# A two-layer trunk on one core: pair sums on POOL, a longer start on one half of the input, one attention pipeline, and tokens on partitions at the end

## The chip, the core and the metric

The kernel runs on one core of a Trainium2 chip. A core has a matrix engine (TensorE, PE in the profile; its weight loads are PEld), a vector engine (VectorE, DVE), a scalar engine (ScalarE, ACT), a general engine (GpSimd, POOL) and a synchronization engine (SyncE, SP) that here only issues DMA transfers. They run side by side, each in the order of its own queue, and wait for one another through semaphores. PE writes its results into eight banks of PSUM, each of 128 partitions by 512 fp32 numbers. The metric is the device time of one execution in microseconds.

## The reference

Input `x` is (1, 512, 1024) in fp32: 512 tokens, 1024 channels. There are two layers; all arithmetic is fp32.

```python
h = x
# layer 0
h = h + conformer_conv(rmsnorm(h, norm_mix[0]), ...)  # a = glu(x @ w_pw1 + b_pw1); y = causal depthwise
                                                      # conv of 31 taps; y = silu(layernorm(y)); y @ w_pw2 + b_pw2
h = h + swiglu_ffn(rmsnorm(h, norm_ffn[0]), w_up[0], w_down[0])   # (silu(x@gate) * (x@up)) @ down, 2816 hidden
k, v = split(rmsnorm(h, norm_kv) @ w_kv)              # 4 heads of 64, shared
# layer 1
q = rmsnorm(h, norm_mix[1]) @ w_q                     # 16 heads of 64
h = h + banded_sink_attention(q, k, v, sinks, rel_bias) @ w_o     # window of 128, blocks of 128 queries
h = h + swiglu_ffn(rmsnorm(h, norm_ffn[1]), w_up[1], w_down[1])
return rmsnorm(h, norm_final)
```

`rmsnorm(x, g)` is `x * rsqrt(mean(x * x) + 1e-6) * g` over the channels. In the attention every block of 128 queries sees its own and the previous block of keys; a learned sink takes part in the maximum and the sum of the softmax.

## The kernel before

**Layout.** `h` is held with channels on partitions: eight tiles of 128 channels by 512 tokens. A matmul takes a 128 x 128 piece of a weight as its stationary operand and a tile of activations, 256 or 512 tokens wide, as its moving one.

**Three matmuls for one product.** Weights come as 512 KB chunks, in the order of a list (`chunk_plan`). Six chunks ahead of use one is fetched by SP; three ahead ACT makes its high part (`whi`, L203) and DVE its low part (`wlo`, L204). Activations are split the same way (L382 and L383 with the norm's gain, L386 and L387 elsewhere). `mm3` then issues three matmuls, high by high (L262), high by low (L263), low by high (L264), in the format fp32r, a cheaper pass than plain fp32. Sums over channels are plain fp32 matmuls with a matrix of ones.

**Layer 0** goes by two halves of 256 tokens as far as its FFN's first part (channel pairs 0 to 4 of 11; the rest runs at 512 tokens). The convolution's 31 taps are shared: DVE does some into a PSUM bank (L611), for the others ACT multiplies (L603) and POOL adds (L604); POOL adds the two results (L615). Tiles go two at a time; such a pair also gets its squares (ACT) and its sums for the layer norm: four matmuls with `ones_m`, two of y and two of the squares (`sums`, L649). Half two's convolution is a generator (`background`) that is advanced by a few steps at each weight chunk while PE runs half one's `pw2` and FFN part; squares follow four steps, sums eight steps behind a pair's end. DVE also has the residual (L731), the eight L383 and the running sum of squares (L340) of half one's norm at that time.

**The norm** is not applied before the FFN. `Rms.step1` sums the squares over channels (L350), DVE adds the epsilon (L352), POOL takes the power of −1/2 (L354), ACT puts the result on a diagonal (L362), and `step2` spreads it to all partitions by a matmul (L375). The evacuation of a pair of FFN channels multiplies by it.

**FFN.** `ffn_up` takes a pair's gate and up products over eight input tiles, in two chunks each of four tiles (`half` 0: tiles 0 to 3, `half` 1: tiles 4 to 7). At 256 tokens the first pair waits for evacuation until the next pair's first half.

**Attention** has 16 units (two head groups x four blocks x two), each a chain of steps: scores on 64 rows (L928), bias and minimum on DVE (L931), exponentials on ACT (L938), division on POOL (L942), transposes by PE (L950) with a split on ACT and DVE, then the product with V. Two row groups of PE, rows 0 to 63 and 64 to 127, hold two heads each. A `pipeline` of eight units lets the steps of five units overlap; it has 12 steps. The first pipeline is advanced within the second half of the query projection (8 steps) and then finished with nothing between, the second one likewise within the output projection's first part.

**The end.** `Fin` finishes the last down projection (channel pairs 9 and 10) half by half of the tokens, with channels on partitions; squares, sums by `ones_c` matmuls, L1072 on POOL, a spread (L1084), and products on DVE and POOL into an output of shape (1024, 512), which the host transposes.

The order of each engine's queue is set by a scheduler that works from the order of the program and its own estimates, with `tc.issue_after` where the code asks for one thing behind another.

Of the kernel before, what the change touches and what calls it, by code (L numbers as in the profile page):

```python
# [10 lines left out]
F32 = mybir.dt.float32  # L11
# [38 lines left out]

def chunk_plan():
# [16 lines left out]
    for _ in range(2):  # L68
        pw2()
        ffn(0, *HALVES0[0])  # L70
# [17 lines left out]
    for hf in range(2):  # L88
        for kp in range(*LAST):
            for g in range(2):  # L90
                plan.append(("down", 1, kp, g))
# [58 lines left out]
def hybrid_trunk(ctx: ExitStack, tc: tile.TileContext, xT, W, prm_in, wdw_in, sinks, relb, onehot, outT):  # L150
# [115 lines left out]
    class Act:  # L266
# [5 lines left out]
        def __getitem__(self, i):  # L272
            a, b = self.q[i // self.per]
            return a[:, i % self.per, :], b[:, i % self.per, :]

# [129 lines left out]
    def down_group(keys, act_of, banks, on_step=None):  # L405
        nk = len(keys)
        w = banks[0].shape[-1]
        for ci, (key, kts) in enumerate(keys):
# [10 lines left out]
            if on_step is not None and ci == nk - 1:  # L419
                on_step()  # L420
                on_step()

    def ffn_part(layer, part, xg, tok, rms, on_h=None):
        lo, hi = (HALVES0, HALVES1)[layer][part]
        hid = ffn_up(layer, lo, hi, xg, tok, rms)
        w = tok.stop - tok.start
        for g in range(2):
            if w == 256:
# [22 lines left out]
    def ffn_up(layer, lo, hi, xg, tok, rms):  # L451
        w = tok.stop - tok.start
        hid = Act(2 * (hi - lo), w)

        def evac(pair, banks):
            rs_bc = rms.step2()
            if w == 256:
# [17 lines left out]
        pending = []  # L475
        for pair in range(lo, hi):
            if w == 256:
                full = [bank(), bank()]
                banks = [b[:, e * w:(e + 1) * w] for b in full for e in range(2)]
            else:  # L480
                full = banks = accs(w)
            for half in range(2):
                for which in range(2):
                    whi, wlo = get("up", layer, pair, half, which)
                    order = [(k, m) for k in range(4) for m in range(2)]
                    if half == 1:
                        order = [(k, m) for m in range(2) for k in range(4)]
                    for k, m in order:
                        sl = slice(m * P, (m + 1) * P)
                        mm3(banks[which * 2 + m], (whi[:, k, sl], wlo[:, k, sl]), cut(xg[half * 4 + k], tok),  # L490
                            half == 0 and k == 0 and opens(m, w), half == 1 and k == 3 and closes(m, w))
                    if half == 0 and which == 1:
                        if w == 512:
                            rms.step1()
                        for p in pending:
                            evac(*p)
                        pending = []
            if w == 256 and pair == lo:
                rms.step1()
                pending.append((pair, full))  # L500
            else:
                evac(pair, full)
# [45 lines left out]
    with tc.tile_pool(name="conv", bufs=2) as cv:  # L548
# [29 lines left out]
        class Half:  # L578
# [246 lines left out]
        x0 = {"ffn0": Act(KT)}  # L825
# [3 lines left out]
        ffn_part(0, 0, x0["ffn0"], HALF[0], n0.rms)  # L829
# [17 lines left out]
    ffn_part(0, 0, x0["ffn0"], HALF[1], n1.rms)  # L847
# [11 lines left out]
    if True:  # L859
# [45 lines left out]
        def q_evac(g, banks):  # L905
# [263 lines left out]
```

## Time and profile before

| | |
|---|---|
| three runs | 1115.78, 1115.91 (median), 1117.93 us |
| the profiled execution | 1115.77 us, of it 1114.0 us from the first to the last instruction (the span) |
| mean clock that TensorE was granted | 0.993 |
| busy share of the span: PE, PEld, DVE, ACT, POOL | 99%, 86%, 59%, 45%, 29% |
| chunks fetched / split | 202 / 194 |
| bytes moved by DMA | 125.00 MB, mean 112 GB/s |

A row of a timeline has its start in microseconds, its length, the engine, the line of the kernel, the operation, what it writes and reads, their form, and the number of instructions folded into the row; brackets at its end give the idle time just before it and what ended that. A row of a group has the count, then the busy time of all, the mean nanoseconds of one, then the idle time before them. A plain fp32 matmul leaves two records in the trace, a matmul in fp32r one. Records of matmuls overlap, so the pace is read from the starts. A slice of the span in the page's second part is 27.9 us.

### The profile page before, as it was taken

The numbers are of one execution on the slowest core, as the hardware profiler recorded it, in microseconds if no ns is written. First come the engines' busy times: TensorE is split into PE (matmuls) and PEld (weight loads), VectorE is DVE, ScalarE is ACT, GpSimd is POOL, SyncE is SP. The second block draws the span as 40 slices with busy tenths as digits, with TensorE's granted clock in tenths as the row PEclk, the third lists the DMA queues.
The fourth block names the chain that finished last, engine by engine and source line by source line (L and its number), as shares of the span: only waits on it lengthen the run. The fifth ranks groups of instructions, "written<-read, shape, count | busy, mean of one in ns | idle before, by whom it ended". The sixth has DMA issues, their size and how long they took to land.

```text
span 1114.0 us, 15803 instructions
## 1 busy us (share of the span) xinstructions
PE 1098.9 (99%) x5994; PEld 955.7 (86%) x5994; DVE 662.3 (59%) x1074; ACT 502.6 (45%) x891; POOL 322.1 (29%) x420
## 2 busy tenths in 40 slices
PE   9999998999999999999999999999999999999997
PEld 8888898999999888888888788888888888888886
DVE  4999999977665454443575686683444333444455
ACT  4786787765543232232343574553322211332233
POOL 4999699700100021110230332241111100110014
PEclk9999998999999999999999999999999999999998
DMA  9227044576655423332322201023233333323332
GB/s 362 100 31 84 25 168 136 183 247 190 189 174 184 135 95 101 105 97 95 95 95 87 75 29 48 30 95 95 95 95 95 97 102 103 96 95 95 95 95 77
DMA packets 40857, 125.00 MB, mean 112 GB/s; under 512 B 4395, under 2 KB 12748, under 8 KB 40780
## 3 DMA queue, kind: packets, MB, share of 16 engines
q1 hardware_dynamic: 40204, 123.55, 36.2%
q8 instruction: 47, 0.77, 0.3%
q10 hardware_dynamic: 576, 0.44, 0.1%
q14 instruction: 30, 0.25, 0.1%
HBM read 118.73 MB, written 5.24 MB: 111 GB/s over the span
## 4 chain that ended last, share of the span: by engine, by line
PE 90%; DVE 5%; ACT 2%; issue 1%; POOL 1%; DMA 0%; SPq 0%; POOLq 0%; DVEq 0%; ACTq 0%
PE bank L263 26%; PE bank L262 26%; PE bank L264 26%; PE bank L562 8%; PE bank L928 1%; DVE quad L383 1%; PE bank L649 1%; ACT pr L603 1%; DVE bank L611 1%; PE bank L950 1%; DVE wlo L204 1%; DMA h<-in_xT_dram 0%; DVE sc L931 0%; PE bank L375 0%; DVE ptl L954 0%
## 5 line engine op out<-in xcount | busy, mean ns | idle before, releaser
L263 PE MATMUL bank<-quad,whi 128*128 128x512 f32 (+1 forms) x1536 | 535.2, 349 | 3.8 <-DVE quad L383 3.7
L262 PE MATMUL bank<-quad,whi 128*128 128x512 f32 (+1 forms) x1536 | 534.8, 350 | 0.5 <-ACT quad L968 0.5
L264 PE MATMUL bank<-quad,wlo 128*128 128x512 f32 (+1 forms) x1536 | 535.1, 348 | 0.0
L204 DVE TENSOR_TENSOR wlo<-raw,whi 128x1024 fp32r<-128x1024 f32 x194 | 262.5, 1354 | 322.4 <-ACT whi L203 312.3
L203 ACT CAST whi<-raw 128x1024 fp32r<-128x1024 f32 x194 | 203.3, 1049 | 360.0 <-PE bank L263 319.3
L263 PEld LDWEIGHTS bank<-quad,whi 128*128 128x128 f32 x1536 | 292.0, 190 | 40.9 <-DVE quad L383 5.0
L262 PEld LDWEIGHTS bank<-quad,whi 128*128 128x128 f32 x1536 | 291.7, 190 | 38.5 <-ACT quad L968 0.9
L264 PEld LDWEIGHTS bank<-quad,wlo 128*128 128x128 f32 x1536 | 292.1, 190 | 36.8 <-issue 0.2
L472 POOL TENSOR_TENSOR tmp<-tmp,tmp 128x512 f32<-128x512 f32 x34 | 48.4, 1425 | 486.7 <-DVE tmp L471 473.1
L604 POOL TENSOR_TENSOR pr<-pr,pr 128x256 f32<-128x256 f32 x208 | 161.6, 825 | 11.0 <-ACT pr L603 11.0
L611 DVE SCALAR_TENSOR_TENSOR bank<-apad,wdw,bank 128x256 f32<-128x256 f32 x248 | 113.2, 485 | 3.6
L562 PE MATMUL bank<-quad,w 128*128 128x256 f32 x512 | 114.2, 382 | 0.6 <-DMA w<-in_W_dram 0.5
L562 PEld LDWEIGHTS bank<-quad,w 128*128 128x128 f32 x512 | 97.4, 191 | 15.4 <-DVE quad L537 1.7
L603 ACT ACTIVATE pr<-apad,wdw 128x256 f32<-128x256 f32 x208 | 99.0, 503 | 20.8 <-POOL pr L604 18.1
L340 POOL TENSOR_TENSOR tmp<-tmp,tmp 128x256 f32<-128x256 f32 (+1 forms) x35 | 38.8, 1109 | 138.6 <-ACT tmp L336 109.1
L470 ACT ACTIVATE tmp<-tmp 128x512 f32<-128x512 f32 x34 | 21.4, 632 | 92.9 <-DVE tmp L469 92.9
L942 POOL TENSOR_SCALAR sc<-sc,sm 128x256 f32<-128x256 f32 (+1 forms) x64 | 30.0, 489 | 79.4 <-DVE sm L940 79.4
L386 ACT CAST quad<-tmp 128x512 fp32r<-128x512 f32 (+1 forms) x50 | 29.1, 586 | 30.4 <-POOL tmp L472 26.6
L471 DVE TENSOR_TENSOR tmp<-bank,rsbc 128x512 f32<-128x512 f32 x34 | 23.5, 691 | 32.4 <-PE bank L264 32.4
L383 DVE SCALAR_TENSOR_TENSOR quad<-h,prm,quad 128x512 fp32r<-128x512 f32 (+1 forms) x40 | 39.5, 1020 | 0.5 <-ACT quad L382 0.4
L938 ACT ACTIVATE sc<-sc,m 128x257 f32<-128x257 f32 (+1 forms) x64 | 30.3, 476 | 15.4 <-DVE m L931 13.7
L387 DVE TENSOR_TENSOR quad<-tmp,quad 128x512 fp32r<-128x512 f32 (+1 forms) x50 | 32.8, 661 | 2.5 <-ACT quad L386 2.5
(140 smaller groups left out, 747.0 us busy)
## 6 DMA issues: line engine op xcount, KB each, us to landing
raw<-in_W_dram SPq DMA_DIRECT2D x202, 512.0 KB, 3.5
w<-in_W_dram SPq DMA_DIRECT2D x15, 512.0 KB, 9.7
fd<-fs SPq DMA_DIRECT2D x1, 3072.0 KB, 33.8
h<-in_xT_dram SPq DMA_DIRECT2D x8, 256.0 KB, 5.9
bias<-fd SPq DMA_DIRECT2D x8, 256.0 KB, 5.5
out_dram<-res SPq DMA_DIRECT2D x14, 128.0 KB, 1.8
w<-in_W_dram SPq DMA_DIRECT2D x2, 256.0 KB, 4.1
out_dram<-res ACTq DMA_DIRECT2D x2, 128.0 KB, 2.7
```

Source lines behind the costliest of these rows:

```text
L203: nc.scalar.copy(hi, r)
L204: lo_engine[0].tensor_sub(lo, r, f32(hi))
L262: nc.tensor.matmul(out, w[0], x[0], start=start, stop=False)
L263: nc.tensor.matmul(out, w[0], x[1], start=False, stop=False)
L264: nc.tensor.matmul(out, w[1], x[0], start=False, stop=stop)
L340: self.eng.tensor_add(sq, self.acc, sq)
L383: nc.vector.scalar_tensor_tensor(dst[1], src, g, f32(dst[0]), op0=ALU.mult, op1=ALU.subtract)
L472: nc.gpsimd.tensor_mul(t2, t1, t2)
L562: mm = nc.tensor.matmul(self.pb[:, w * W2:(w + 1) * W2], w1[ct][:, w, k, :], x[k] if x else xg[k][:, tok], start=k == 0, stop=k == KT - 1)
L603: on_act = nc.scalar.mul(pr, a[:, j:j + W2], tap(j))
L604: on_pool = nc.gpsimd.tensor_add(pr, acc, pr)
L611: on_dve = nc.vector.scalar_tensor_tensor(yt if i == nd - 1 else c, src, tap(i), c if i else self.shift, op0=ALU.mult, op1=ALU.add)
```

## The change

Five things are changed.

1. For half two of the convolution (`hf` is 1), `sums` has POOL add the two y tiles of a pair into a new tile `yy` (one buffer) and the two squares in place; one matmul with `ones_m` for each sum takes the place of two.
2. FFN part one of half two is made in a `twin` form: the high and low parts of an activation stand side by side (`Pairs`), so that the high weights multiply both in one 512-wide matmul, and the low weights the high part in one of 256 (`mm2`). The two column halves of a bank are added in the evacuation.
3. FFN part one of half one takes its chunks `ahead`: first tiles 0 to 3 of pairs 0 and 1, then tiles 4 to 7 of both. Pairs 0 and 1 are evacuated after the latter.
4. Attention is one pipeline of 16 units and 20 steps: 8 within the second half of the query projection, 4 with nothing between, 8 within the output projection's first part. The second half's queries are evacuated bank by bank. The twelve score matmuls of a unit are held in strict turn between the two row groups by `issue_after`, behind a tiny matmul (1 x 1) into one of their banks.
5. At the end the activations are the stationary operand and the weights the moving one, 512 wide, so that tokens lie on partitions: a `Block` of 128 tokens gets its part of `h` by eight transposes into PSUM, then the products on top. ACT squares with a running sum, POOL takes the power for 128 tokens at once, and ACT and DVE multiply by it. `norm_final` is fetched by SP as a broadcast of 512 KB. The last four chunks are fetched once, not twice (198 fetched and 190 split).

```diff
-    def ffn(layer, lo, hi):
-        for pair in range(lo, hi):
-            for half in range(2):
-                for which in range(2):
-                    plan.append(("up", layer, pair, half, which))
+    def ffn(layer, lo, hi, ahead=False):
+        for pair, half in up_order(lo, hi, ahead):     # ahead: o[1], o[2] = o[2], o[1]
+            for which in range(2):
+                plan.append(("up", layer, pair, half, which))
...
+    def mm2(out, w, x, start, stop):
+        first, second = (w[0], x, out), (w[1], x[:, 0, :], out[:, 0, :])
+        if stop:
+            first, second = second, first
+        nc.tensor.matmul(first[2], first[0], first[1], start=start, stop=False)
+        nc.tensor.matmul(second[2], second[0], second[1], start=False, stop=stop)
...
+                for which, t in enumerate((t1, t2)):
+                    for m in range(2):
+                        b = banks[which * 2 + m]
+                        tm = t[:, m * w:(m + 1) * w]
+                        nc.scalar.copy(tm, b[:, 1, :])
+                        nc.vector.tensor_add(tm, b[:, 0, :], tm)
...
+                if self.hf:
+                    for f, (t, u) in enumerate(((self.y[:, 2 * p, :], self.y[:, 2 * p + 1, :]), self.sq)):
+                        both = u
+                        if f == 0:
+                            both = cv.tile([P, W2], F32, tag="yy", name=uid("yy"), bufs=1)
+                        nc.gpsimd.tensor_add(both, t, u)
+                        mm = nc.tensor.matmul(self.st[:, f * W2:(f + 1) * W2], ones_m, both,
+                                              start=p == 0 and f == 0, stop=p == KT // 2 - 1 and f == 1)
+                    return mm.ins
...
-        ffn_part(0, 0, x0["ffn0"], HALF[0], n0.rms)
+        ffn_part(0, 0, x0["ffn0"], HALF[0], n0.rms, ahead=True)
...
-    ffn_part(0, 0, x0["ffn0"], HALF[1], n1.rms)
+    ffn_part(0, 0, x0["ffn0"], HALF[1], n1.rms, twin=True)
...
+            mm = nc.tensor.matmul(pbs[1][0:1, 0, 0:1], ones_c, ones_c, start=True, stop=True)
...
-                        nc.tensor.matmul(pbs[g][:, e, :], qs[gp][a][rows[g], j, qt],
-                                         kq[rows[g], b, gp, k0:k0 + BAND], start=a + b == 0, stop=a == 1)
+                        with tc.issue_after(mm.ins):
+                            mm = nc.tensor.matmul(pbs[g][:, e, :], qs[gp][a][rows[g], j, qt],
+                                                  kq[rows[g], b, gp, k0:k0 + BAND], start=a + b == 0, stop=a == 1)
...
-            units = [unit(gp, jp, n) for n in range(NBLK) for jp in range(2)]
+            units = [unit(gp, jp, n) for gp in range(2) for n in range(NBLK) for jp in range(2)]
...
+            for i in range(KT):
+                c = (i % 4) * P
+                nc.tensor.matmul(self.banks[i // 4][:, c:c + P], h[i][:, self.tok], ident, is_transpose=True,
+                                 start=i % 4 == 0, stop=False)
...
+                for n, (x, w) in enumerate(((a[0], whi), (a[0], wlo), (a[1], whi))):
+                    nc.tensor.matmul(self.banks[g], x, w[:, k, :], start=False, stop=kp == LAST[1] - 1 and k == 1 and n == 2)
...
+            nc.scalar.activation(sq, b, AF.Square, accum_out=ss[:, g:g + 1])
...
+                nc.gpsimd.tensor_tensor(rs, ss[:, 3:4], mhalf[:, 0:1], op=ALU.pow)
```

The scheduler moves more than these lines say. Line numbers of the changed kernel are higher: taps are L686 (DVE) and L679 (POOL), splits L209, L409 stands for L383 and L366 for L340, L267 to L269 for the three matmuls, L401 for the spread, L690 for the sum of both parts of y.

DVE where half one's norm input is made, before (`wlo_1732` is the low part of the fifth FFN chunk):

```order
L204 TENSOR_TENSOR wlo_1686<-raw_1529,whi_1685 128x1024
L383 SCALAR_TENSOR_TENSOR quad_1318<-h,prm,quad_1317 128x256
L340 TENSOR_TENSOR tmp_1606<-tmp_1477,tmp_1606 128x256
L383 SCALAR_TENSOR_TENSOR quad_1318<-h,prm,quad_1317 128x256 x2
L340 TENSOR_TENSOR tmp_1612<-tmp_1606,tmp_1612 128x256
L383 SCALAR_TENSOR_TENSOR quad_1318<-h,prm,quad_1317 128x256
L340 TENSOR_TENSOR tmp_1618<-tmp_1612,tmp_1618 128x256
L340 TENSOR_TENSOR tmp_1624<-tmp_1618,tmp_1624 128x256
L204 TENSOR_TENSOR wlo_1732<-raw_1573,whi_1731 128x1024
L204 TENSOR_TENSOR wlo_1770<-raw_1633,whi_1769 128x1024
```

And in the changed kernel (`wlo_1736` is the same place in the list of chunks):

```order
L209 TENSOR_TENSOR wlo_1688<-raw_1530,whi_1687 128x1024
L409 SCALAR_TENSOR_TENSOR quad_1317<-h,prm,quad_1317 128x256
L366 TENSOR_TENSOR tmp_1613<-tmp_1607,tmp_1613 128x256
L686 SCALAR_TENSOR_TENSOR bank_1489<-apad_158,wdw,bank_1489 128x256
L409 SCALAR_TENSOR_TENSOR quad_1318<-h,prm,quad_1318 128x256 x2
L366 TENSOR_TENSOR tmp_1619<-tmp_1613,tmp_1619 128x256
L686 SCALAR_TENSOR_TENSOR y_1020<-apad_157,wdw,bank_1489 128x256
L686 SCALAR_TENSOR_TENSOR y_1020<-apad_158,wdw,bank_1489 128x256
L686 SCALAR_TENSOR_TENSOR bank_1857<-apad_159,wdw,bank_1270 128x256
L366 TENSOR_TENSOR tmp_1625<-tmp_1619,tmp_1625 128x256
L209 TENSOR_TENSOR wlo_1736<-raw_1574,whi_1735 128x1024
L686 SCALAR_TENSOR_TENSOR bank_1857<-apad_160,wdw,bank_1270 128x256
```

Taps now stand between the norm's rows, the first tap of the next pair among them; the fifth chunk's low part still follows all of the norm's rows.

POOL behind pair 2's last tap (`y_1020` is half two's convolution result), before:

```order
L604 TENSOR_TENSOR pr_1785<-pr_1777,pr_1785 128x256
L615 TENSOR_TENSOR y_1020<-y_1020,pr_1781 128x256
L615 TENSOR_TENSOR y_1020<-y_1020,pr_1785 128x256
L354 TENSOR_TENSOR rs_1818<-ms_1816,mhalf 128x2
L604 TENSOR_TENSOR pr_1911<-pr_1866,pr_1911 128x256
```

and in the changed kernel, where L726 is the new pair of adds:

```order
L679 TENSOR_TENSOR pr_1789<-pr_1781,pr_1789 128x256
L690 TENSOR_TENSOR y_1020<-y_1020,pr_1785 128x256
L690 TENSOR_TENSOR y_1020<-y_1020,pr_1789 128x256
L679 TENSOR_TENSOR pr_1904<-pr_1858,pr_1904 128x256
L679 TENSOR_TENSOR pr_1908<-pr_1861,pr_1908 128x256
L726 TENSOR_TENSOR yy_2109<-y_1020 128x256
L679 TENSOR_TENSOR pr_1912<-pr_1904,pr_1912 128x256
L679 TENSOR_TENSOR pr_1916<-pr_1908,pr_1916 128x256
L380 TENSOR_TENSOR rs_1893<-ms_1891,mhalf 128x2
L679 TENSOR_TENSOR pr_1950<-pr_1912,pr_1950 128x256
L726 TENSOR_TENSOR sq_2015<-sq_2013,sq_2015 128x256
```

Taps of pair 3 and the norm's power now stand between pair 2's y and the two new adds.

PE at pair 2's sums, in the changed kernel:

```order
L267 MATMUL bank_1732<-quad_1318,whi_1853 128x256
L268 MATMUL bank_1732<-quad_1318,whi_1853 128x256
L269 MATMUL bank_1732<-quad_1318,wlo_1854 128x256
L727 MATMUL bank_1376<-yy_2109,ones_m 128x256
L727 MATMUL bank_1376<-sq_2015,ones_m 128x256
L401 MATMUL bank_1982<-tmp_1895,ones_m 128x256
L267 MATMUL bank_1997<-quad_1315,whi_1900 128x256
```

Before, the spread of the norm (L375) stood 77 rows of matmuls ahead of the pair's four sums; now the two sums stand directly ahead of it, in front of the third pair's first chunk.

More of the change, by code (lines that the diff above doesn't have):

```diff
@@ L48, with up_order @@
 NPARAM = _c
+def up_order(lo, hi, ahead):
+    o = [(pair, half) for pair in range(lo, hi) for half in range(2)]
+    if ahead:
+        o[1], o[2] = o[2], o[1]
+    return o
 def chunk_plan():
@@ L149, in hybrid_trunk @@
 @with_exitstack
[L150 removed]
+def hybrid_trunk(ctx: ExitStack, tc: tile.TileContext, xT, W, prm_in, wdw_in, sinks, relb, onehot, fin, out):
     nc = tc.nc
@@ L473, in evac @@
                 split(hid[2 * (pair - lo) + m], t2)
[L475 to L498, printed above, removed]
```

297 lines of the change are left out of this document (159 added, 138 removed).

## The prediction, made before the changed kernel ran

> **What bounds the kernel now.** I read the page's busy times first, then the chain of waits, then busy times by stretches, then the timelines of the stretches where TensorE (PE) is not full.
>
> ```profile
> PE 1098.9 (99%) x5994; PEld 955.7 (86%) x5994; DVE 662.3 (59%) x1074; ACT 502.6 (45%) x891; POOL 322.1 (29%) x420
> PEclk9999998999999999999999999999999999999998
> PE 90%; DVE 5%; ACT 2%; issue 1%; POOL 1%; DMA 0%; SPq 0%; POOLq 0%; DVEq 0%; ACTq 0%
> ```
>
> PE is busy for 99% of the span and carries 90% of the chain. So the time is PE's work, plus the few places where PE stands still or is clocked down, plus the end. Only slice 7 of the clock (167 to 195 us) and the last one fall short. By stretches (length, then busy time and count of PE, PEld, DVE, ACT, POOL, then granted clock, DMA share, GB/s):
>
> ```profile
> 160.00:180.00 20.00, 17.03 (x110) 16.18 (x109) 19.82 (x27) 17.16 (x36) 20.00 (x21) 0.83 0.50 171
> 180.00:220.00 40.00, 40.00 (x328) 39.74 (x328) 36.05 (x54) 30.95 (x54) 33.46 (x34) 1.00 0.54 170
> 270.00:290.00 20.00, 20.00 (x169) 20.00 (x168) 17.82 (x23) 12.69 (x23) 5.78 (x7) 1.00 0.58 182
> 640.00:660.00 20.00, 19.66 (x140) 17.18 (x139) 19.05 (x55) 16.40 (x49) 9.09 (x20) 1.00 0.14 49
> ```
>
> At 160 to 180 us PE is idle for 20.00 − 17.03 = 2.97 us and the clock costs 20 × 0.17 = 3.4 us: 6.4 us are lost, the largest prize in the program. DVE (19.82) and POOL (20.00) are both full there. At 180 to 220 us PE loses nothing, and POOL still has 6.5 us free.
>
> **The convolution sums and the new order of chunks, 150 to 230 us.** These belong together, because both decide what PE waits for in one stretch.
>
> ```profile
> 161.06 0.47 PE L262 MATMUL bank<-quad,whi 128*128 128x256 f32 x1
> 169.16 0.39 PE L263 MATMUL bank<-quad,whi 128*128 128x256 f32 x1 [1.88 <-DVE quad L383]
> 170.90 0.58 PE L263 MATMUL bank<-quad,whi 128*128 128x256 f32 x1 [0.99 <-DVE quad L383]
> 168.16 0.94 DVE L383 SCALAR_TENSOR_TENSOR quad<-h,prm,quad 128x256 fp32r<-128x256 f32 x1
> 175.13 3.42 DVE L204 TENSOR_TENSOR wlo<-raw,whi 128x1024 fp32r<-128x1024 f32 x2
> 197.54 1.73 PE bank L649 x8
> 225.18 1.73 PE bank L649 x8
> ```
>
> A plain fp32 matmul leaves two records, so the eight of a pair's sums are four matmuls: 1.73 / 4 = 0.43 us each. Half two loses eight of its sixteen: 8 × 0.43 = 3.45 us of PE work gone.
>
> The stall is PE at tiles 4 to 7 of the normalized input, which DVE (L383) finishes late. With the new order PE first does four chunks that need tiles 0 to 3 alone: 4 × 24 matmuls × 0.12 us (next part) = 11.5 us of work before it needs the rest; now the two chunks from 161.06 are all it has. But the fifth chunk also needs its own low part. In the changed order on DVE that split still stands behind every tile's L383 and L340 work, with one tap more ahead of it. Before, the two splits ran from 175.13, so the first was done near 176.8; one tap (36.05 / 54 bounds it by 0.67 us) makes that about 177.3. PE comes there at 161.06 − 0.86 (two sums of pair 1 saved) + 11.5 = 171.7 us. So the wait changes its name, from the tile to the low weights, and I do not book the 6.4 us.
>
> The second half is POOL's queue.
>
> ```profile
> 156.55 26.37 POOL L604 TENSOR_TENSOR pr<-pr,pr 128x256 f32<-128x256 f32 x26
> 182.88 2.41 POOL L615 TENSOR_TENSOR y<-y,pr 128x256 f32<-128x256 f32 x2
> 185.25 0.71 POOL L354 TENSOR_TENSOR rs<-ms,mhalf 128x2 f32<-128x2 f32 x1
> L604 POOL TENSOR_TENSOR pr<-pr,pr 128x256 f32<-128x256 f32 x208 | 161.6, 825 | 11.0 <-ACT pr L603 11.0
> 220.54 2.42 POOL L615 TENSOR_TENSOR y<-y,pr 128x256 f32<-128x256 f32 x2 [7.09 <-DVE y L611]
> ```
>
> A tap of POOL takes 26.37 / 26 = 1.01 us here, and I take 0.9 us for a 128x256 add of two tiles (the mean over all taps is 0.825). POOL was running without a gap from 156.55. In the changed order pair 2's squares come out of POOL at 156.55 + 26.37 (taps) + 1.8 (pair 1's two adds) + 2.41 (two y) + 2.0 (two taps) + 0.9 (yy) + 2.0 + 0.71 (pow) + 1.0 (tap) + 0.9 (squares) = 194.6 us. On PE, the last sum of pair 2 now stands 7.5 us of work nearer the start than the first one did: 1.7 us is the four matmuls saved at pairs 0 and 1, and 5.8 us its move ahead by some 50 rows. So PE gets there at 197.54 − 7.5 = 190.0 us if the old stall stays as it is, and at 183.6 if it goes: in both cases it waits for POOL until 194.6. Behind that sum on PE stand the spread of the norm (L401) and all further chunks, and ACT and DVE wait for their banks. From there to any later point PE has 7.5 us of moved or saved work to count, less the whole saving of 3.45: 194.6 + 7.5 − 3.45 − 197.54 = +1.1 us. I take **+1.0 us**. From below the bound is −3.45 − 6.4 = −9.9 (no stall left), from above two further stretches at half clock, +6.8, and a later POOL.
>
> The trace's half clock lasts one stretch worth 3.4 us, after PE had been idle 1.88 and 0.99 us within 2.7. The Trainium skill ("TensorE: Matmul & The Clock Gate", Part 1) says that the gate looks at free-running windows of about 3.4 us and halves the clock after an idle one; by that figure a cold window would cost an estimated 1.7 us, half of what this row shows, so the measurement decides and the row's 3.4 us is used.
>
> **The twin form, half two's first FFN part.** 240 triples (5 pairs × 4 chunks × 8, plus 10 chunks × 8) become a 512-wide and a 256-wide matmul each.
>
> ```profile
> 269.75 0.28 PE L264 MATMUL bank<-quad,wlo 128*128 128x256 f32 x1
> 289.91 0.28 PE L264 MATMUL bank<-quad,wlo 128*128 128x256 f32 x1
> 399.71 0.39 PE L262 MATMUL bank<-quad,whi 128*128 128x512 f32 x1
> 419.88 0.39 PE L264 MATMUL bank<-quad,wlo 128*128 128x512 f32 x1
> ```
>
> Starts give the pace: 20.16 us over 168 matmuls is 0.120 us at 256 wide, 20.17 over 89 is 0.2266 at 512. A triple goes from 0.360 to 0.3466, so 240 × 13.4 ns = 3.2 us go. The evacuation grows (four copies, four adds, two products on POOL); at 270 to 290 us DVE is busy 17.82 of 20, ACT 12.69 and POOL 5.78, so there is room beside PE, least of it on DVE, where two products with the norm go and four adds come. The norm is now asked for after half a pair, not a whole one, and its spread stands on PE only a few triples behind; a wait there is −0 to 1.5 us. I take **−2.4 us**, bounds −3.2 and 0.
>
> **Attention.** PE runs scores of 64 rows, two groups at once.
>
> ```profile
> 616.25 0.90 PE bank L928 x12
> 628.36 0.90 PE bank L928 x6
> 629.68 0.90 PE bank L928 x6
> 749.62 0.79 PE bank L350 x8
> 697.19 0.57 issue
> 699.68 0.88 ACT sc L938 x3
> 700.59 1.17 ACT sc L938 x5
> ```
>
> Twelve scores in turn between the two row groups take 0.90 us; six of one group by themselves take 0.90 too. Where the order separated the groups a unit costs 0.88 us more. About four and a half of sixteen units read like 628.36: strict turn saves 4.5 × 0.88 = 3.95 us. The tiny matmul ahead of each unit is plain fp32 of one column; four of them took 0.79 us (L350 with 8 records), so 16 × 0.2 = 3.2 us at most and about 1 us if only its issue shows; I take 2.4. One pipeline has one fill and one drain. The chain leaves PE for 2.6 us at the joint (issue and ACT, last three rows). But four bare steps remain, each with a full unit, and DVE is at 19.05 of 20 us at 640 to 660: I book −0.3, bounds 0 and −2.6. Sum −3.95 + 2.4 − 0.3 = **−1.8 us**, bounds −5.6 and +2 (separation as before, all dummies paid: 3.2, less 1 of the joint).
>
> **The end.** 192 matmuls of 256 (23.0 us) and a spread (0.43) become 96 of 512 (21.75) and 32 transposes.
>
> ```profile
> 709.93 0.87 PE bank L950 x8
> 1101.05 0.28 PE L264 MATMUL bank<-quad,wlo 128*128 128x256 f32 x1
> 1104.75 0.71 POOL L1072 TENSOR_TENSOR rs<-ms,mhalf 128x2 f32<-128x2 f32 x1
> 1108.53 1.41 POOL L1100 TENSOR_TENSOR res<-res,tmp 128x256 f32<-128x256 f32 x2 [3.08 <-ACT tmp L1093]
> 1109.29 1.04 ACTq L1096 DMA_DIRECT2D out_dram<-res  x2
> L336 ACT ACTIVATE tmp<-h 128x512 f32<-128x512 f32 x16 | 9.9, 616 | 0.0
> L603 ACT ACTIVATE pr<-apad,wdw 128x256 f32<-128x256 f32 x208 | 99.0, 503 | 20.8 <-POOL pr L604 18.1
> L352 DVE TENSOR_SCALAR ms<-bank 128x2 f32<-128x2 f32 x4 | 0.6, 156 | 5.6 <-PE bank L350 5.6
> L938 ACT ACTIVATION_READ_ACCUMULATOR sc<-sc,m 128x1 f32 x64 | 12.0, 188 | 0.0
> ```
>
> Transposes cost 32 × 0.109 = 3.5 us, so PE's work grows by 21.75 + 3.5 − 23.4 = +1.8, and I add 0.5 for the changes between transposes and fp32r. Behind the last matmul there are 1114.0 − 1101.34 = 12.66 us now (sums, pow, spread, copy, product, store). After: square of a bank 0.62 and its sum 0.19, a tiny DVE step 0.16 (L352), pow 0.71, two ACT products of 256 columns 1.0 (L603), hand-overs 0.5, then, as now, from the last store's issue (it begins about 0.4 us before the ACTq row ends at 1110.33) to the end, 4.1: 7.3 us. So −12.66 + 7.3 + 2.3 = **−3.0 us**, bounds −4.5 and −1.5. The gain's broadcast (512 KB) and four fewer loads lie under FFN work, with DMA 0.14 to 0.5 busy: nothing.
>
> The Trainium skill ("TensorE: Matmul & The Clock Gate", Part 4) puts a transpose at about 275 ns in a kernel and says that transposes do not count as busy for the clock gate. By that, 32 would cost an estimated 8.8 us and the end would gain nothing (+2.3); this trace has eight in 0.87 us, so I keep 3.5.
>
> **The sum** against the profiled execution (1115.77 us, 1.77 of it outside the span; 0.14 under the median shown): +1.0 − 2.4 − 1.8 − 3.0 = −6.2, so **1109.6 us**. About 0.2%, 2.2 us, is what a measurement of this kernel tells from no change.
>
> **The rivals.**
> 1. *The stall goes.* The fifth split comes out earlier than its place says, POOL's adds are done when PE arrives, and only the last sums bind: y of pair 3 is done by DVE near 220.5 now (POOL waits 7.09 for it), and DVE with 36.05 of 40 could bring it 4 us ahead, which lets PE be at most 5 us early at 225.18. For it: the four chunks ahead are real work. Against: DVE's 19.82 of 20. A term of −5 in place of +1.0: 1103.6.
> 2. *One more stretch at half clock* behind the wait for POOL, which is longer (4.6 us or more) than the idle that set off the first: +3.4, 1113.0.
> 3. *Attention and the twin form give nothing*, because waits for DVE fill what PE saves (19.05 of 20): −6.2 + 4.2 = −2.0, 1113.8.
> 4. *Slower: POOL becomes what PE waits for.* Its adds wait for taps whose products ACT makes, and each microsecond on the 194.6 is one on the end. If the squares come at 200 us (+5.4), a half-clock stretch (+3.4) goes with it: −6.2 + 8.8 = +2.6, 1118.4. It decides from about 199.6 us on. Against: POOL has been busy without gaps, so 194.6 is not far off.
>
> **How the numbers follow.** Forecast 0.50 (own range 1106.5 to 1112.5), rival 1 0.14, rival 2 0.17, rival 3 0.11, rival 4 0.08. Faster than 1113.7: all of the forecast but 0.01, rival 1, two thirds of rival 2, half of rival 3: 0.79. Within: 0.13. Slower than 1118.1: most of rival 4 and the tails, 0.08. The range 1103.5 to 1115.0 leaves out rival 4, the lower part of rival 1 and the upper tail of 3.
>
> **What would show it.** At 165 to 180 us: PE's wait named by a low-weight split, and none by L409. Near 194 us: a PE wait for POOL's L726, then the clock of the stretch. In 255 to 330 us: pairs of starts 0.2266 + 0.12 apart. In attention: all scores as x12 in 0.90. Behind the last matmul: 7.3 us. The prediction is wrong if no wait for POOL shows before 200 us (then lower), if a second clock stretch follows it (higher), or if the tiny matmuls cost over 0.3 us each.

## The result, and the profile after

The changed kernel takes **1109.1 us** (median of 5, 1108.14 to 1109.72); the kernel before, timed again beside it, 1115.99 us. The ratio is 0.9939, with a 95% interval of 0.9927 to 0.9950, so it is faster by 0.6%, or 6.9 us. The forecast was 1109.6. The sum was right to half a microsecond, but three of its four terms were not: two savings were booked 1 and 2 us too small, and one loss 1.6 us too small.

The page of the changed kernel (busy times, clock in 40 slices, chain by engine):

```profile
span 1107.3 us, 15193 instructions
PE 1087.1 (98%) x5680; PEld 929.5 (84%) x5680; DVE 662.5 (60%) x1077; ACT 507.1 (46%) x914; POOL 337.8 (31%) x433
PEclk9999999999999999999999999999999999999999
PE 88%; issue 4%; DVE 3%; ACT 3%; POOL 2%; DMA 0%; SPq 0%; POOLq 0%
```

PE has 11.8 us less work than before, and the kernel is 6.9 us faster. Four spreads that stand at the same place in both programs cut the time into stretches. In the chain of waits of before (start, length, what) they are half one's first spread, half two's layer norm, keys and values, and the last FFN:

```profile
56.42 0.43 PE bank L375 x2
237.75 0.86 PE bank L680 x2
585.14 0.86 PE bank L375 x2
761.47 0.86 PE bank L375 x2
```

and in the chain of the changed kernel:

```profile
57.26 0.43 PE bank L401 x2
241.14 0.86 PE bank L764 x2
586.61 0.86 PE bank L401 x2
759.90 0.86 PE bank L401 x2
```

| stretch | before | after | difference | term of the prediction |
|---|---|---|---|---|
| to half one's first spread | 56.42 | 57.26 | +0.8 | none (its scatter: 56.5 to 58.9 in the runs below) |
| to half two's layer norm: convolution, half one's FFN | 181.33 | 183.88 | **+2.6** | +1.0 |
| to keys and values: twin form | 347.39 | 345.47 | **−1.9** | −2.4 |
| to the last FFN: attention | 176.33 | 173.29 | **−3.0** | −1.8 |
| to the end: FFN and the new end | 352.5 | 347.4 | **−5.1** | −3.0 |

Five of the runs below leave the first part of the changed kernel as it is (no twin form, attention of before, end of before, no tiny matmul, and the changed kernel once more). Their stretch to half two's layer norm is 183.7 to 184.7 us, so the 183.88 of this one profile is no outlier, and a difference of 0.5 us in that row is not more than its scatter.

Where the first term went is seen in PE's rows from 160 to 200 us (the timeline of the changed kernel, rows with an idle time ahead of them):

```profile
161.88 0.70 PE L727 MATMUL bank<-yy,ones_m 128*128 128x256 f32 x2 [1.15 <-POOL yy L726]
164.93 0.70 PE L727 MATMUL bank<-sq,ones_m 128*128 128x256 f32 x2 [1.41 <-POOL sq L726]
176.16 0.39 PE L269 MATMUL bank<-quad,wlo 128*128 128x256 f32 x1 [0.83 <-DVE wlo L209]
190.42 0.70 PE L727 MATMUL bank<-yy,ones_m 128*128 128x256 f32 x2 [2.28 <-POOL yy L726]
194.81 1.22 PE L727 MATMUL bank<-sq,ones_m 128*128 128x256 f32 x2 [3.69 <-POOL sq L726]
```

The stall for tiles 4 to 7 is gone. In its place PE waits four times for POOL's new adds, 8.5 us in all. POOL's timeline around the last two of them:

```profile
185.88 1.44 POOL L690 TENSOR_TENSOR y<-y,pr 128x256 f32<-128x256 f32 x2
187.27 2.39 POOL L679 TENSOR_TENSOR pr<-pr,pr 128x256 f32<-128x256 f32 x2
189.63 0.74 POOL L726 TENSOR_TENSOR yy<-y 128x256 f32<-128x256 f32 x1
190.31 2.40 POOL L679 TENSOR_TENSOR pr<-pr,pr 128x256 f32<-128x256 f32 x2
192.68 0.70 POOL L380 TENSOR_TENSOR rs<-ms,mhalf 128x2 f32<-128x2 f32 x1
193.36 0.72 POOL L679 TENSOR_TENSOR pr<-pr,pr 128x256 f32<-128x256 f32 x1
194.05 0.71 POOL L726 TENSOR_TENSOR sq<-sq,sq 128x256 f32<-128x256 f32 x1
```

The squares are out at 194.76; the prediction counted 194.6 through the queue. The half clock came back as well, 20 us later, behind these waits (columns as in the prediction):

```profile
160.00:180.00 20.00, 16.61 (x132) 15.90 (x131) 19.96 (x29) 16.33 (x33) 20.00 (x20) 1.00 0.46 164
180.00:200.00 20.00, 14.02 (x95) 13.06 (x94) 15.18 (x23) 14.34 (x28) 20.00 (x22) 0.83 0.44 147
```

And the end, on the timeline of the changed kernel:

```profile
1101.21 0.39 PE L1133 MATMUL bank<-whi,quad 128*128 128x512 f32 x1
1101.64 0.60 ACT L1138 ACTIVATE sq<-bank 128x512 f32<-128x512 f32 x1 [2.03 <-PE bank L1133]
1102.13 0.19 ACT L1138 ACTIVATION_READ_ACCUMULATOR sq<-bank 128x1 f32 x1
1102.36 0.16 DVE L1142 SCALAR_TENSOR_TENSOR ss<-ss 128x1 f32<-128x1 f32 x1 [1.95 <-ACT sq L1138]
1102.60 0.55 POOL L1144 TENSOR_TENSOR rs<-ss,mhalf 128x1 f32<-128x1 f32 x1 [5.79 <-DVE ss L1142]
1103.17 0.91 ACT L1157 ACTIVATE hg<-hg,rs 128x256 f32<-128x256 f32 x2 [0.85 <-POOL rs L1144]
1103.71 0.83 ACTq L1158 DMA_DIRECT2D out_dram<-hg  x2
```

The last matmul ends at 1101.60, the span at 1107.3: 5.7 us, where there were 12.7.

### The profile page after: what moved, and what is told of

Its sections match the earlier page's. It is cut to its first block, busy times and chain, and to the rows that moved or that the text cites. A ratio compares the mean times of both kernels' runs of the same rounds, so it can differ in the third digit from the quotient of the medians.

```text
span 1107.3 us, 15193 instructions
## 1 busy us (share of the span) xinstructions
PE 1087.1 (98%) x5680; PEld 929.5 (84%) x5680; DVE 662.5 (60%) x1077; ACT 507.1 (46%) x914; POOL 337.8 (31%) x433
## 4 chain that ended last, share of the span: by engine, by line
PE 88%; issue 4%; DVE 3%; ACT 3%; POOL 2%; DMA 0%; SPq 0%; POOLq 0%
PE bank L267 22%; PE bank L268 22%; PE bank L269 22%; PE bank L637 8%; PE bank L299 5%; PE bank L300 3%; PE bank L1133 1%; PE bank L1016 1%; POOL pr L679 1%; ACT pr L678 1%; PE bank L1038 1%; DVE quad L409 1%; PE bank L733 1%; DVE bank L686 0%; DMA h<-in_xT_dram 0%
## 5 line engine op out<-in xcount | busy, mean ns | idle before, releaser
L209 DVE TENSOR_TENSOR wlo<-raw,whi 128x1024 fp32r<-128x1024 f32 x190 | 264.8, 1395 | 310.4 <-ACT whi L208 304.3
L269 PE MATMUL bank<-quad,wlo 128*128 128x512 f32 (+1 forms) x1232 | 448.8, 364 | 0.8 <-DVE wlo L209 0.8
L268 PE MATMUL bank<-quad,whi 128*128 128x512 f32 (+1 forms) x1232 | 448.1, 364 | 0.9 <-DVE quad L409 0.9
L267 PE MATMUL bank<-quad,whi 128*128 128x512 f32 (+1 forms) x1232 | 448.6, 366 | 0.0
L208 ACT CAST whi<-raw 128x1024 fp32r<-128x1024 f32 x190 | 199.3, 1049 | 333.6 <-PE bank L268 283.5
L269 PEld LDWEIGHTS bank<-quad,wlo 128*128 128x128 f32 x1232 | 233.0, 189 | 37.4 <-DVE wlo L209 1.0
L268 PEld LDWEIGHTS bank<-quad,whi 128*128 128x128 f32 x1232 | 233.1, 189 | 37.2 <-DVE quad L409 1.3
L267 PEld LDWEIGHTS bank<-quad,whi 128*128 128x128 f32 x1232 | 233.0, 189 | 37.0 <-issue 0.5
L679 POOL TENSOR_TENSOR pr<-pr,pr 128x256 f32<-128x256 f32 x208 | 160.8, 809 | 5.3 <-ACT pr L678 5.3
L686 DVE SCALAR_TENSOR_TENSOR bank<-apad,wdw,bank 128x256 f32<-128x256 f32 x248 | 113.2, 484 | 3.5
L366 POOL TENSOR_TENSOR tmp<-tmp,tmp 128x256 f32<-128x256 f32 (+1 forms) x35 | 38.0, 1085 | 151.9 <-ACT tmp L362 122.6
L299 PE MATMUL bank<-quad,whi 128*128 128x512 f32 x212 | 75.9, 398 | 0.0
L300 PE MATMUL bank<-quad,wlo 128*128 128x256 f32 x212 | 59.3, 280 | 0.0
L299 PEld LDWEIGHTS bank<-quad,whi 128*128 128x128 f32 x212 | 39.7, 188 | 8.4
```

The costliest lines, as they stand in the source:

```text
L208: nc.scalar.copy(hi, r)
L209: lo_engine[0].tensor_sub(lo, r, f32(hi))
L267: nc.tensor.matmul(out, w[0], x[0], start=start, stop=False)
L268: nc.tensor.matmul(out, w[0], x[1], start=False, stop=False)
L269: nc.tensor.matmul(out, w[1], x[0], start=False, stop=stop)
L299: nc.tensor.matmul(first[2], first[0], first[1], start=start, stop=False)
```

## The experiments

All were timed in five rounds beside the kernel before, whose median was 1115.9 to 1116.4 us in these. Each is the changed kernel but for the edit shown. "Stretch" is the time between the spreads of the table above, taken from each run's profile.

### Which of the two first parts costs what

**Sums of half two on PE again, order ahead kept:**

```diff
-                if self.hf:
+                if self.hf > 1:
```

> The changed kernel, but half two's sums are made by PE as before (four matmuls for a pair, no adds on POOL); chunks ahead stay. Theory (POOL's whole queue is late, the adds are only a part of it): PE's waits for the two adds (2.6 us at pair 1, 6.0 us at pair 2) go, but the norm's spread L401 behind pair 2 then waits for POOL's pow, which stands behind taps, until about 193 us, and a half-clock stretch may follow. 3.45 us of PE work come back. Time about 1107.3 us, within 2 of the changed kernel's 1109.1. Rival A (the adds alone are what PE waits for): no wait over 1 us between 180 and 200 us, clock 1.00 there, time about 1103.5. Rival B (the adds cost nothing and save 3.45 us): 1112.5.

Measured: 1109.43 us (1108.81 to 1110.38), the same as the changed kernel; the first stretch is 184.05 (changed 183.88). The gain of the theory does not show in the stretch, so its 1107.3 was 2 us too low, and rival A's 1103.5 and rival B's 1112.5 are far off. (The profiled run, the slowest of the five, also has a step of half clock at 581 us, and its second stretch is 1.5 us longer.) PE's rows show that each wait taken away has a successor:

```profile
176.90 0.38 PE L269 MATMUL bank<-quad,wlo 128*128 128x256 f32 x1 [3.27 <-DVE wlo L209]
192.66 0.70 PE L401 MATMUL bank<-tmp,ones_m 128*128 128x256 f32 x2 [0.57 <-ACT tmp L388]
199.82 0.39 PE L267 MATMUL bank<-quad,whi 128*128 128x256 f32 x1 [1.48 <-ACT rsbc L395]
211.09 0.39 PE L269 MATMUL bank<-quad,wlo 128*128 128x256 f32 x1 [1.29 <-DVE wlo L209]
```

The first is the fifth chunk's low part, the wait that the prediction saw coming at 172 to 177 us; in the changed kernel the waits at pair 1 had used up most of it (0.83 left). The spread waits behind POOL's pow as the theory said, but for 0.6 us, not for the whole way. So the adds are not alone what PE waits for.

**Chunks pair by pair again, POOL's adds kept** (`ahead` is left out in the plan and in the call):

```diff
-        ffn(0, *HALVES0[0], ahead=hf == 0)
+        ffn(0, *HALVES0[0])
...
-        ffn_part(0, 0, x0["ffn0"], HALF[0], n0.rms, ahead=True)
+        ffn_part(0, 0, x0["ffn0"], HALF[0], n0.rms)
```

> The changed kernel, but half one's FFN takes its chunks pair by pair as before; POOL's adds stay. Theory: the stall for tiles 4 to 7 comes back at 167 to 177 us (about 3 us of idle and 3.4 us of half clock), but it hides the 2.6 us of pair 1, and pair 2's sums stand late enough on PE (85 matmuls behind the spread) to wait for nothing. The stretch to half two's spread loses 6.4 us and saves 3.45, against the changed kernel's loss of 12.8 less 3.45: about 1103.5 us, the order ahead is what costs. Rival A (adds alone cost): 1108 to 1110, since PE still waits for L726 at pair 2. Rival B (the order ahead is a gain): 1112 or more.

Measured: 1107.42 us (1107.24 to 1108.35), first stretch 182.63. The direction of the theory, and less than half of its 5.6 us. Pair 2's sums wait for nothing, as it said. But the stall for tiles 4 to 7 did not come back: it is 0.10 us, PE having waited for the adds of pair 1 before it (1.13 and 1.41 us, at 161 and 164 us). On POOL these two adds, 3.4 us, stand in a queue without gaps ahead of the norm's power, and PE then waits for the spread, and later for a low part (0.95 us at 211 us) and for pair 3's adds (0.34 and 0.97):

```profile
182.98 1.69 POOL L380 TENSOR_TENSOR rs<-ms,mhalf 128x2 f32<-128x2 f32 x1
185.45 0.70 PE L401 MATMUL bank<-tmp,ones_m 128*128 128x256 f32 x2 [2.20 <-ACT tmp L388]
```

**Neither:**

> The changed kernel without both: sums of half two on PE and chunks pair by pair. The first 240 us are then those of the kernel before. Theory: half two's layer-norm spread at 237.7 us plus the start's own scatter, a time of 1106.5 us (changed kernel less the 2.6 us that it lost there by the two profiles). If the loss there was only the scatter of one profile: 1109. If one of the two parts is a gain by itself, e1 or e2 is under this run, by 3 us for e2 in the theory.

Measured: 1106.59 us (1105.87 to 1108.44), first stretch 181.13: the theory's number, and the stretch of the kernel before (181.33). The first two parts together cost the changed kernel 2.5 us. The three runs don't add up (adds alone 181.13 to 182.63, order alone to 184.05, both to 183.88), because the waits of the one hide those of the other, as the rows above show: without the adds PE waits 3.27 us for the fifth low part, with them 0.83.

**The sums' matmuls later.** The two adds stay at step 8 behind a pair, the matmuls go to step 16:

```diff
-                    due += [(4, ...squares(p)), (8, ...sums(p))]
+                    due += [(4, ...squares(p)), (8, ...adds(p)), (16, ...sums(p))]
```

> The changed kernel with POOL's adds where they are, but their matmuls eight steps of the convolution later, so PE meets pair 1's and the squares of pair 2 later (the y sum of pair 2 still stands ahead of the spread). Theory (POOL's queue): the waits of 2.6 us at pair 1 and of 3.7 us for pair 2's squares go, but the spread L401 waits for POOL's pow until about 194.5, so the end moves by 1 to 2 us only: about 1107.5 us. Rival A (adds alone): 1103 to 1104, clock 1.00 from 180 to 200 us.

Measured: 1110.89 us (1109.04 to 1111.81), first stretch 185.56; slower, against both expectations. The waits at pair 1 and for pair 2's squares went, and came back at once:

```profile
175.83 0.39 PE L269 MATMUL bank<-quad,wlo 128*128 128x256 f32 x1 [3.28 <-DVE wlo L209]
195.58 0.79 PE L723 MATMUL bank<-yy,ones_m 128*128 128x256 f32 x1 [6.29 <-POOL yy L739]
193.21 0.71 POOL L380 TENSOR_TENSOR rs<-ms,mhalf 128x2 f32<-128x2 f32 x1
193.89 1.64 POOL L739 TENSOR_TENSOR yy<-y 128x256 f32<-128x256 f32 x1
```

PE came to pair 2's y sum, which the scheduler had left ahead of the spread, at 189.3 us, no earlier than in the changed kernel (188.1). What moved is POOL: the scheduler put its y rows behind more taps and the norm's power ahead of the add, so that `yy` is ready at 195.5 us and not at 190.4, and PE waited 6.3 us in one piece. So this run did not keep POOL's queue as it was, and says nothing on PE's order alone.

### The other terms, undone one at a time

**No twin form** (`twin=True` is left out of the call).

> The changed kernel, but half two's first FFN part is made by three 256-wide matmuls as before. Theory (the twin form saves 3.2 us of PE work and pays 0.8 to 1.3 of it back in waits): from the spread of half two's layer norm to the key and value part the stretch is 1.9 to 2.4 us longer than in the changed kernel, time about 1111.3. Rival (the saving is hidden by DVE's evacuation): 1109.1, no difference.

Measured: 1111.32 us (1110.23 to 1112.04), 2.2 us over the changed kernel; its second stretch is 347.39, to the hundredth that of before, against 345.47. The twin form is worth 1.9 us by the stretch. The waits of the theory do not show; where the rest of the 3.2 us went is told below.

**The attention of before** (two pipelines, queries evacuated together, no turn, no tiny matmul).

> The changed kernel with the two pipelines of before, queries evacuated together, no turn and no tiny matmul. By the prediction's term the stretch from the key and value spread to the FFN's is 1.8 us longer: 1110.9; by the two profiles 3.0 us: 1112.1. Rival (DVE sets the pace of the bare steps whatever the order): 1109.1.

Measured: 1112.15 us (1111.85 to 1112.9), the attention stretch 176.34 against 173.29. All 3.0 us come from there.

**The end of before** (the class `Fin`, its order of chunks and its output).

> The changed kernel with the end of before (channels on partitions, half by half). By the prediction's term 3.0 us longer: 1112.1. By the two profiles 5.2 us: PE 1.7 us shorter up to the last matmul, and 12.7 instead of 5.7 us behind it: 1114.3. Rival (the shorter end is scatter of stores in one profile): 1111 or less.

Measured: 1114.66 us (median of 11, 1113.47 to 1116.1), 5.6 us over the changed kernel; the last stretch is 352.5 as before, 5.1 us longer than the changed kernel's 347.4. The new end is the largest part of the change.

**The strict turn without the tiny matmul:**

```diff
-            mm = nc.tensor.matmul(pbs[1][0:1, 0, 0:1], ones_c, ones_c, start=True, stop=True)
+            mm = None
...
-                        with tc.issue_after(mm.ins):
+                        with tc.issue_after(mm.ins) if mm else nullcontext():
```

> The changed kernel with the strict turn but without the tiny matmul ahead of each unit. The prediction booked 2.4 us for sixteen of them: 1106.7, if all of it is on PE's path. Rival (the tiny matmul takes the wait for a free bank that the first score would take, and costs about 1 us in all): 1108.1. Slower than 1109.5 if it is what keeps the groups in turn, which would show as scores x6 in 0.90 us.

Measured: 1109.01 us (1108.56 to 1109.13), no difference in time; but the attention stretch is 172.36 against 173.29, 0.93 us or 58 ns net for each of sixteen. In this profile the first stretch was longer (184.53) and the half clock lasted 10.2 us, not 6.8, which hid most of it. In the chain of waits about half of the units still read x12 in 0.90, and in the others one score runs ahead by itself:

```profile
618.12 0.90 PE bank L1016 x12
630.23 0.31 PE bank L1016
632.12 0.91 PE bank L1016 x9
```

In the changed kernel such a unit reads:

```profile
631.58 0.90 PE bank L1016 x12
650.58 0.91 PE bank L1016 x12
```

So the tiny matmul does keep the first score with the others, but in these profiles it costs more than that is worth; the turn of the rest holds without it.

### Putting it together

**Neither of the first two parts, and no tiny matmul:**

> Sums of half two on PE, chunks pair by pair, strict turn without the tiny matmul; twin form, one pipeline and the new end stay. If the parts add up as the earlier profiles say (2.8 us for the two first together in the first 240 us, 0.9 us for sixteen tiny matmuls of 58 ns): 1106.6 - 0.9 = 1105.7. If the gain of the two was scatter: 1108.

Measured: **1105.89 us** (1105.78 to 1106.46), ratio to before 0.9909 (0.9893 to 0.9924). The parts add up, and this beats the changed kernel by 3.2 us, and by 3.7 us when both are timed side by side (the last run below).

**Pair 0's sums alone on POOL, on top of that** (`if self.hf and p == 0`):

> As the run without both and without the tiny matmul, but pair 0's sums are added on POOL (two adds, two matmuls less on PE). Theory (each add on POOL pushes all behind it): PE saves 0.86 us before the stall for tiles 4 to 7, which waits for DVE and so eats the saving, and POOL's queue is 1.5 us later behind it, so the spread waits 1 to 2 us for the pow or nothing: 1105.7 to 1107.5. Rival (only adds of pairs 1 to 3 cost): 1104.8.

Measured: 1105.70 us (1105.33 to 1106.31), no difference; first stretch 181.39. Four matmuls became two and bought nothing: at 211 us PE now waits for a low part from DVE, where the longest such wait of the run without this was 0.05 us.

```profile
211.21 0.39 PE L269 MATMUL bank<-quad,wlo 128*128 128x256 f32 x1 [0.65 <-DVE wlo L209]
```

**Four sums of squares behind the last L409, on top of the run before last:**

```diff
+            if self.eng is not nc.vector or i < 4:
                 self.rms.add(h[i][:, self.tok])
+            elif i == KT - 1:
+                with tc.issue_after(low):          # low: the last tile's L409
+                    for j in range(4, KT):
+                        self.rms.add(h[j][:, self.tok])
```

> As the run without both and without the tiny matmul, with one change of order on DVE: the sums of squares of tiles 4 to 7 of half one's norm (four L366 of about 0.95 us) are issued behind the last L409. Theory (the stall at 170 us is DVE's queue ahead of tiles 5 to 7): the second wait of 1 us goes and what half clock hides behind it, the first of 1.9 us stays; if the clock is cut for one step of 3.4 us and not for two, 1.7 us more go: 1102.9 to 1104.7. Rival (the fourth and fifth low parts bind next): 1105.7.

Measured: 1105.48 us (1105.26 to 1106.19), no difference that can be told from 1105.89; first stretch 181.30. That is the rival's number, not the theory's. The stall did shrink, and the spread then waited in its place:

```profile
169.44 0.39 PE L268 MATMUL bank<-quad,whi 128*128 128x256 f32 x1 [1.34 <-DVE quad L409]
170.32 0.39 PE L268 MATMUL bank<-quad,whi 128*128 128x256 f32 x1 [0.26 <-DVE quad L409]
171.20 0.39 PE L268 MATMUL bank<-quad,whi 128*128 128x256 f32 x1 [0.25 <-DVE quad L409]
187.82 0.70 PE L401 MATMUL bank<-tmp,ones_m 128*128 128x256 f32 x2 [1.34 <-ACT tmp L388]
```

The runs without the order ahead and with at most pair 0's adds on POOL all end the first stretch within 181.1 to 181.4, as does the kernel before. They are not alike on the way. From half one's first spread to the FFN matmul behind pair 2's sums, at about 199 us, PE takes 142.7 us before and 141.7 to 141.9 in these last three runs; to the one behind pair 3's sums, at about 227 us, it is 170.3 and 170.2 to 170.4. What they gain, 0.7 to 0.9 us, is gone between, at 205 to 212 us, where matmuls with a low part from DVE start late. DVE is full there (stretches of the last run):

```profile
184.00:204.00 20.00, 18.66 (x148) 18.20 (x147) 16.12 (x24) 16.89 (x33) 20.00 (x22) 1.00 0.48 155
204.00:224.00 20.00, 19.99 (x163) 19.45 (x162) 19.96 (x30) 13.63 (x21) 12.90 (x12) 1.00 0.59 184
```

DVE at 19.96 of 20, with POOL waiting 7 us for its y at the end of that stretch, is what I take to set the 181 us now; that was read from these rows and not tried by taking work from DVE. Nor need a full DVE be only its own work: in one profile, the changed kernel's, POOL's add of two y tiles took 1.71 us at 160 us and 0.74 at 189.63, so operations of DVE and POOL may hold one another up, and no run here took that apart.

**The changed kernel once more**, beside these three:

> The changed kernel as it is, beside the three others on the same chip: 1109.1 by its first timing, so 3 to 4 us over the run without both and without the tiny matmul. Its wait for POOL's L726 near 190 us and one half-clock stretch behind it appear again, if they are of the program and not of one execution.

Measured: 1109.55 us (1108.9 to 1113.34), with PE's waits of 1.11, 1.41, 0.82, 2.27 and 3.70 us at the same places (1.15, 1.41, 0.83, 2.28 and 3.69 in the first profile), and two steps of the clock behind them. They belong to the program, not to one execution.

## Why the prediction was right, and where it was not

**Sums and order, +1.0: measured +2.6, and −2.5 when both are undone.** The main step held: the squares leave POOL at 194.76 (194.6 counted), PE waits there, and the order ahead does not earn the 6.4 us. That the count hit to 0.2 us is luck: POOL reached its 26 taps at 158.04 and not at 156.55, pair 1's two adds took 3.4 us for 1.8, and the taps and the two y took 2.7 us less than counted. Three sizes failed. The count was made for pair 2 alone, and the same queue holds PE for 1.15 and 1.41 us at pair 1. The 5.6 us of waiting for the fifth low part, seen in the order of DVE, is 0.83 here because PE is late already, and 3.3 when the adds are gone. And rival 2 happened together with the forecast: a stretch at half clock behind the wait; the prediction had named such a stretch as a sign that the time comes out higher. It cost about 2 us and not 3.4, since it began at 192.0 and 2.8 of its 6.8 us lay under the wait itself. By their starts, PE's matmuls from 160 us to the end of the stretch are late by 12.4 us in all against a pace of 0.120 us (0.216 for a record of a plain fp32 one), and by 6.4 before; up to 160 us both kernels are level. So 12.4 − 6.4 − 3.45 saved = +2.55, the measured +2.6.

**Rival 1 (the stall goes, −5)** had half of its mechanism: the stall went. What stood against it in the prediction, DVE's 19.82 of 20, is also what seems to bind when both parts are taken out. **Rival 4 (slower by POOL's queue)** had the place and the mechanism right, and the point from which it decides, 199.6 us, was not reached.

**Twin form, −2.4: −1.9** by the profiles and +2.2 when undone. Here the pace was mis-sized, not the waits. Just behind the spread pairs of starts in the changed kernel are 0.3475 us apart (299.08 to 301.86 us, eight pairs), as computed; but over the 207 pairs from 299.08 to 371.94 us it is 0.352, and 240 × (0.360 − 0.352) = 1.9 us, all that was measured. From the start of a 512-wide matmul of this part to the next start are 0.235 us, where the prediction took 0.2266 from others. The 0.8 us that it gave away for waits on DVE stood in for that by chance.

**Attention, −1.8: −3.0.** The separated scores went as counted; all fourteen groups in the chain read x12 in 0.90 or 0.91. The term for the tiny matmul was too large: 2.4 booked, 0.93 measured, net of what it does for the order. It was bounded by four L350 matmuls in 0.79 us, whose stationary operand has 128 columns, and these have one: the load of that operand takes 192 ns there and 81 ns here (medians). That this is the reason was not tried. The prediction's 1 us "if only its issue shows" was the better number. That is 1.5 us, more than the 1.2 by which the term was short. The 0.3 booked for the joint does not show: PE is idle for 1.4 us from 616 to 735 us before and for 1.5 after.

**The end, −3.0: −5.1 to −5.6.** PE's work from the first matmul of the end to the last one grew by 1.7 us (1077.69 to 1101.33 before, 1076.29 to 1101.60 after), against +2.3 booked: no cost shows at the change from transposes to fp32r, where 0.5 was added. Behind the last matmul 5.7 us were measured for 7.3. Pow takes 0.55 us on one column (0.71 on two), the hand-overs are 0.02 to 0.08 us each, and from the end of the last store's issue (1104.54) to the end of the span there are 2.8 us, where there were 3.7. So the mechanism held, and the term was mis-sized in two places: 7.3 us behind the last matmul where 5.7 were measured, and the 0.5 for a change of kind that does not show.

**Transposes.** The prediction weighed a rule of the Trainium skill ("TensorE: Matmul & The Clock Gate", Part 4, about 275 ns a transpose) against the row of eight in 0.87. The trace of the changed kernel has both: the 32 at the end have a mean record of 272 ns (the group of L1123), and sixteen of them stand in 1.75 us of the chain, 0.109 each. So here the page's figure (which it gives for bf16) is how long one lasts, and the time is set by how often one starts.

**The likeliest number was right partly by chance.** Errors of +1.6, +0.5, −1.2 and −2.1 nearly cancel, and 0.8 of start scatter came on top. Two readings in it do not hold, without moving the sum: the two waits ahead of the half clock lie within 3.6 us and not 2.7 (167.28 to 170.90), and 36.05 / 54 is a mean and bounds nothing.

## What to carry to other kernels

Where two engines were full for a stretch (DVE 19.8 of 20, POOL 20.0), less work on a third one bought nothing, even though that one carries 90% of the chain: its waits only changed their names. Work that is moved to a full engine should be priced by its place in that engine's queue, at each of its places, and then by what else stands behind it (here the norm's power). And of a bundle of edits each one is worth a run with it undone: two of these five cost 2.5 us together, while the bundle was faster by 6.9.

## What the runs showed of the hardware

- The stretches at half clock last 3.41, 6.83 or 10.24 us in the clock records (the one that the end of the program cuts off left out), so steps of 3.41. The row of 6.83 us in the profile before was two steps, not one. That agrees with the Trainium skill ("TensorE: Matmul & The Clock Gate", Part 1), which the prediction had set aside: its window of about 3.4 us, 1.7 us lost in each, is the unit. The stretches at full clock between two cuts are whole multiples too (13.65 us, four steps, in the run with the sums later; 928.42 us, 272 steps, before), so the steps lie on a grid that does not start with a wait.
- By the records of the matmuls, what a step does goes with PE's idle time in the step before it. Every half-clock step that began a stretch, but for one, came behind a step in which PE was idle for 1.72 us or more, in several runs for no more than 1.9, so the step need not be idle throughout. It was followed by another one at half clock wherever PE was idle for 0.45 us or more in it, and by full clock where that was 0.09 or less. The limit is not sharp in these records: three steps with 1.76 or 1.77 us idle had full clock behind them. Before, and in the run without both parts and without the tiny matmul (columns as in the prediction):

```profile
167.13:170.54 3.41, 0.89 (x6) 0.54 (x4) 3.41 (x4) 3.07 (x9) 3.41 (x5) 1.00 0.65 213
170.54:173.95 3.41, 2.96 (x12) 2.66 (x13) 3.41 (x5) 2.69 (x6) 3.41 (x5) 0.50 0.18 72
168.77:172.18 3.41, 0.75 (x5) 0.55 (x5) 3.41 (x5) 3.06 (x8) 3.41 (x4) 1.00 0.62 193
172.18:175.59 3.41, 3.32 (x14) 3.02 (x14) 3.41 (x4) 2.69 (x6) 3.41 (x5) 0.50 0.05 20
```

  Both have waits of 1.9 and 1.0 us. Before, 0.45 us of them reached into the half-clock step and a second one followed; in the other run 0.09 us did, and none followed (granted clock 0.83 and 0.91 at 160 to 180 us). So it was the place of the wait on the grid that differed; no run set that place.
- The exception is a step of 3.41 us at 581 us in the run with the sums on PE, which made its second stretch 346.96 instead of 345.47. PE was idle for 0.86 us in the step before it, and 0.83 to 0.87 us at the same place in eight other profiles, where no cut followed. What set it off stays open.
